# Gates taken out of the retention and made in seven products of sums of blocks, with the attention's output projection ahead of them

## The chip, the cores and the metric

The kernel runs on one core of one Trainium2 chip. The metric is the device time of one execution, in microseconds (us); a kernel's time is the median of its runs. The engines are named as in the profile: PE (TensorE matmuls) and PEld (its weight loads), DVE (VectorE), ACT (ScalarE), POOL (GpSimd) and SP (SyncE, which issues nearly all DMA transfers of this kernel, in program order).

## The reference

One layer of a hybrid model: a block of neighbourhood attention and a block of retention share one input projection, each is projected back, both are merged by gates, and a gated MLP follows. Cut to the part that the change touches (1024 tokens, width 1024, 4 retention heads with values 256 wide, 1024 columns for each gate):

```python
hx = _modulate(_rmsnorm(x, norm1_g[l]), sh1, sc1)
(xq, xk, xv, xrq, xrk, xrv, xrg, xga, xgb) = jnp.split(hx @ w_in[l], IN_OFFSETS, axis=-1)
...
o_ret_x, _, _ = _bi_retention(q_r, k_r, _heads(xrv, RET_HEADS), ret_log_decay_fwd[l], ret_log_decay_bwd[l], s_f, s_b)
o_ret = _ret_output(o_ret_x, xrg)
...
merged = jax.nn.sigmoid(gate_na) * (o_na @ w_proj_na) + jax.nn.sigmoid(gate_ret) * (o_ret @ w_proj_ret)
return merged @ w_out
```

There are thus three gates, each `hx` (1024 x 1024) times a weight of 1024 x 1024: `xrg` (weight `w_rg`), with which the retention's output is multiplied after a SiLU, and `xga`, `xgb` (weight `w_gate`, branches 0 and 1), sigmoids on the two projected branches.

## The kernel before

Every operand of a matmul is held as a sum of two, high and low (`split`, L83: ACT copies to the high part, DVE subtracts for the low one), and every product is made of three matmuls: high by high, high by low, low by high (`chain`, L103, and `mm3`, L120). A weight block of 128 x 512 comes through `wload` (L95): SP loads it into one of three `raw` buffers, and `split` writes it into one of six `wc` buffers. A DMA is issued on SP in the order in which the program is written, or later where a buffer has to come free first. The tiles are given out by pools with a fixed number of buffers, and each engine works through its instructions in order.

The parts that matter here, in the order of the program:

- **Retention.** For each of the four heads there are ten `front` slots (two blocks of context, eight of tokens) that make queries, keys and values, and four `gate` slots (L1156) that make the head's gate with `w_rg`, SiLU included, into `sg`. A `slot` (L1234) issues three pieces of its main work and between them the steps of another generator: the mixing (`Mix`: `mix_a`, `mix_b`, `mix_c`) of a head whose front is complete. So a head's mixing starts in its own gate slots (three of them carry a step) and goes on in the next head's front slots. `mix_b` normalises a block of 128 tokens (bn_stats, bn_aggr and a power on POOL), `mix_c` transposes it and multiplies it by `sg`, and stores it to `d_oret` in DRAM.
- **Tail.** The last head's mixing has three gates as filler (`tail`, `gate_fill`). They are three of the eight merge gates that were made early and spilled to `d_gate`, those of the output blocks `db` 0 to 3; the other five are made during the attention.
- **Gates and projections** (L1300 to L1377). The eight remaining merge gates (`db` 4 to 7, both branches; tiles `g`), with the loads of the spilled ones between them; beside them eight transposed blocks of the attention's output (`tpn`, L1347, loaded from `d_ona`) and the generator `down_sums`, which loads 44 blocks of `w_down`, makes 44 differences on POOL (`pj`, L1317) and stores them to `d_w`. Then the attention's output projection with `w_pna` (`pn`, L1374), multiplied by its gate, and between its blocks the retention's output comes back from `d_oret` and is split to `orr` (L1370).
- **Merge.** The retention's projection with `w_pret` (`pr`, L1393), times its gate, plus the other branch. Then `w_out` and the MLP. Its up projection already uses seven products of sums of blocks in place of eight products (a class with a method `step` of seven cases).

Products with a two by two division of both operands into blocks come, in that form, as seven products instead of eight; the sums of weight blocks are made on POOL (`s1` to `s4`), those of the moving operand once (T1 to T4), and those of the results when they leave PSUM.

## Time and profile before

| | us |
|---|---|
| median of three runs | 1797.33 (1794.11 and 1798.88 the others) |
| profiled execution, its own time | 1797.5 |
| span of the profiled execution, first to last instruction | 1795.7 |
| mean granted clock of TensorE over the span | 0.990 |

Busy time of the engines in the stretches that the change rebuilds, and the share of the DMA engines' time:

| stretch (us from the start of the span) | PE | DVE | ACT | POOL | granted clock | DMA |
|---|---|---|---|---|---|---|
| 470 to 813, retention from the second head to the end of its tail | 343.00 | 208.46 | 131.61 | 77.50 | 1.00 | 0.22 |
| 813 to 905, merge gates, transposes, `down_sums` | 90.90 | 14.77 | 28.11 | 52.33 | 1.00 | 0.91 |
| 905 to 949, projection `pn`, `orr` | 40.54 | 28.08 | 18.95 | 5.86 | 0.96 | 0.75 |
| 949 to 1036, projection `pr` and merge | 87.00 | 42.14 | 22.18 | 40.62 | 1.00 | 0.29 |

How to read the profile: an engine's busy time over a stretch, against the length of the stretch, says how far it is from being full there. "Idle before" of an instruction is the time for which its engine had nothing to do ahead of it, and the name behind the arrow is what ended that time. A line such as L84 is a line of the kernel; L84 and L85 are the two halves of `split`, wherever it is called.

### The profile page before, as it was taken

The numbers are of one execution on the slowest core, as the hardware profiler recorded it, in microseconds if no ns is written. First come the engines' busy times: TensorE is split into PE (matmuls) and PEld (weight loads), VectorE is DVE, ScalarE is ACT, GpSimd is POOL, SyncE is SP. The second block draws the span as 40 slices with busy tenths as digits, with TensorE's granted clock in tenths as the row PEclk, the third lists the DMA queues.
The fourth block names the chain that finished last, engine by engine and source line by source line (L and its number), as shares of the span: only waits on it lengthen the run. The fifth ranks groups of instructions, "written<-read, shape, count | busy, mean of one in ns | idle before, by whom it ended". The sixth has DMA issues, their size and how long they took to land.

```text
span 1795.7 us, 24565 instructions
## 1 busy us (share of the span) xinstructions
PE 1746.7 (97%) x8477; PEld 1450.1 (81%) x8477; DVE 1216.9 (68%) x2386; ACT 821.2 (46%) x1768; POOL 520.8 (29%) x445
## 2 busy tenths in 40 slices
PE   8799999999999999999999999989999999999997
PEld 4588888888888888888778878878888888788886
DVE  5978887765656666551254646869989989875755
ACT  5666666652524343432342223544444444554444
POOL 2600000001222212125422610065545555211444
PEclk9899999999999999999999999999999999999999
DMA  9134334330303030238982333642232233486753
GB/s 356 52 113 128 105 113 148 119 98 9 95 16 100 19 91 24 74 91 285 318 262 88 88 136 134 235 160 88 90 116 88 97 122 104 163 284 193 240 168 149
DMA packets 128031, 240.64 MB, mean 134 GB/s; under 512 B 14593, under 2 KB 27041, under 8 KB 127905
## 3 DMA queue, kind: packets, MB, share of 16 engines
q1 hardware_dynamic: 127904, 239.06, 41.0%
q8 instruction: 67, 1.10, 0.3%
q14 instruction: 60, 0.48, 0.1%
HBM read 179.48 MB, written 56.90 MB: 132 GB/s over the span
## 4 chain that ended last, share of the span: by engine, by line
PE 74%; DVE 6%; issue 6%; DMA 6%; POOL 4%; ACT 3%; SPq 1%; POOLq 0%; ACTq 0%; DVEq 0%
PE u L1628 18%; PE mm L110 5%; PE mm L111 5%; PE mm L112 5%; PE y L1628 4%; PE mm L121 4%; PE mm L123 4%; PE mm L122 4%; PE R L509 2%; PE ptp L491 2%; PE om L121 1%; PE om L122 1%; PE om L123 1%; DVE wc L85 1%; DMA raw<-in_w_out 1%
## 5 line engine op out<-in xcount | busy, mean ns | idle before, releaser
L1628 PE MATMUL u<-T,wc 128*128 128x512 f32 x960 | 227.0, 392 | 5.3 <-ACT pu L1605 5.0
L1628 PEld LDWEIGHTS u<-T,wc 128*128 128x128 f32 x960 | 180.5, 189 | 46.3 <-ACT pu L1605 8.8
L1628 PE MATMUL y<-wc,ahl 128*128 128x512 f32 x924 | 212.2, 392 | 3.3 <-DVE wc L85 1.8
L1628 PEld LDWEIGHTS y<-wc,ahl 128*128 128x128 f32 x924 | 174.5, 189 | 40.8 <-DVE wc L85 2.5
L111 PE MATMUL mm<-low,wc 128*128 128x512 f32 (+1 forms) x456 | 174.1, 382 | 0.0
L85 DVE TENSOR_TENSOR wc<-ur,wc 128x512 fp32r<-128x512 f32 x137 | 122.6, 896 | 66.3 <-ACT wc L84 66.3
L110 PE MATMUL mm<-hx,wc 128*128 128x512 f32 x392 | 157.8, 403 | 0.3 <-DVE vc L219 0.3
L85 DVE TENSOR_TENSOR wc<-raw,wc 128x512 fp32r<-128x512 f32 x140 | 104.8, 753 | 75.5 <-ACT wc L84 75.1
L112 PE MATMUL mm<-hx,wc 128*128 128x512 f32 x392 | 155.1, 396 | 0.0
L84 ACT CAST wc<-ur 128x512 fp32r<-128x512 f32 x137 | 85.1, 622 | 129.7 <-PE y L1628 72.1
L84 ACT CAST wc<-raw 128x512 fp32r<-128x512 f32 x140 | 86.8, 621 | 72.5 <-DMA raw<-in_w_gate 22.6
L1628 PE MATMUL u<-h2a,wc 128*128 128x512 f32 x480 | 112.3, 389 | 0.7 <-DVE pu L1613 0.7
L1628 PEld LDWEIGHTS u<-h2a,wc 128*128 128x128 f32 x480 | 90.0, 188 | 19.8 <-DVE pu L1613 1.1
L111 PEld LDWEIGHTS mm<-low,wc 128*128 128x128 f32 x456 | 86.1, 189 | 11.3
L84 ACT CAST wc<-s 128x512 fp32r<-128x512 f32 x80 | 49.6, 622 | 91.9 <-PE u L1628 87.0
L123 PE MATMUL mm<-wc,low 128*128 128x512 f32 (+1 forms) x240 | 91.2, 380 | 0.0
L85 DVE TENSOR_TENSOR wc<-s,wc 128x512 fp32r<-128x512 f32 x80 | 83.4, 1044 | 3.7 <-ACT wc L84 3.4
L112 PEld LDWEIGHTS mm<-hx,wc 128*128 128x128 f32 x392 | 73.8, 188 | 13.6
L110 PEld LDWEIGHTS mm<-hx,wc 128*128 128x128 f32 x392 | 73.9, 189 | 12.1 <-PE c L123 0.7
L1351 POOL TENSOR_TENSOR col<-col,bcol 128x32 f32<-128x32 f32 x1 | 0.3, 253 | 281.6 <-DVE aw L536 281.6
L121 PE MATMUL mm<-wc,hx 128*128 128x512 f32 x192 | 75.2, 392 | 0.7 <-ACT r L1103 0.7
L122 PE MATMUL mm<-wc,hx 128*128 128x512 f32 x192 | 75.1, 391 | 0.0
(380 smaller groups left out, 4424.6 us busy)
## 6 DMA issues: line engine op xcount, KB each, us to landing
ur<-in_w_up SPq DMA_DIRECT2D x80, 256.0 KB, 2.8
ur<-d_a SPq DMA_DIRECT2D x77, 256.0 KB, 3.2
aw<-in_w_ada SPq DMA_DIRECT2D x32, 512.0 KB, 3.3
pj<-in_w_down SPq DMA_DIRECT2D x44, 256.0 KB, 4.6
d_w<-pj SPq DMA_DIRECT2D x44, 256.0 KB, 4.3
d_a<-sa SPq DMA_DIRECT2D x44, 256.0 KB, 2.0
ur<-d_w SPq DMA_DIRECT2D x44, 256.0 KB, 3.9
d_a<-at SPq DMA_DIRECT2D x33, 256.0 KB, 2.6
```

The costliest lines, as they stand in the source:

```text
L84: act.copy(hi, src)
L85: (lo_eng or vec).tensor_tensor(lo, src, hi.bitcast(F32), ALU.subtract)
L110: pe.matmul(out, wh, xh, start=k == 0, stop=False)
L111: pe.matmul(out, wh, xl, start=False, stop=False)
L112: pe.matmul(out, wl, xh, start=False, stop=k == n - 1)
L121: pe.matmul(out, ah, bh, start=first, stop=False)
L122: pe.matmul(out, ah, bl, start=False, stop=False)
L123: pe.matmul(out, al, bh, start=False, stop=last)
L491: pe.transpose(tp[:, c], self.Pm[h][:, c * P : (c + 1) * P], ident)
L509: pe.matmul(R[:, h], self.pair.V[:, g, h].rearrange("p a b -> p (a b)"), self.PT[h][:, c].rearrange("p a b -> p (a b)"), start=c == 0, sto ...
L1351: pool.tensor_tensor(col[:, 16:48], col[:, 16:48], bcol[:, 16:48], ALU.add)
L1628: pe.matmul(out, a, b, start=first and n == 0, stop=last and n == 2, skip_group_check=True)
```

## The change

The retention no longer makes its gates: `gate` is gone, `mix_c` copies the transposed block to DRAM as it is, and the mixing of a head rides along in slots 1 to 9 of the next head's front and slot 0 of the one after. `v` gets buffers of its own for the context blocks (`c0`, `c1`). The filler of the tail comes in pieces of six matmuls instead of nine (`STEP`).

Behind the retention come, in this order: the eight transposes `tpn`; the attention's output projection `pn` for all eight `db`, stored to a new `d_pn` (times the gate for `db` 0 to 3, whose gates were spilled, without it for `db` 4 to 7), and beside it `hx_sums`, which forms the sums T1 to T4 of the blocks of `hx` on POOL and DVE and splits them; then the class `Gates`, eight units of seven products of twelve matmuls each: four retention heads (`ret`, `w_rg`) and the merge gates of `db` 4 to 7 (`merge`, `w_gate`, both branches in one unit). The steps of neighbouring units are interleaved, and `down_sums` advances at every fifth step. A unit's results go through SiLU or sigmoid, are multiplied by the retention's output from `d_oret` or the projection from `d_pn` where that applies, and are stored to `d_orr`, `d_pn` or `d_gate`. Behind the units, 16 tiles of `d_orr` are loaded and split to `orr`, and 16 tiles each of `d_pn` and `d_gate` loaded to `sg`. The projection with `w_pret` and all behind it are as before. The up projection's class becomes `Up`, with the common part in `Seven`; its instructions and their order stay.

PE has 8463 instructions before and 8367 after, ACT 1600 and 1673, DVE 2348 and 2412, POOL 450 and 498, SP 866 and 946.

PE, end of the retention, before: the last transposes of the mixing (`tpo`) stand among matmuls of a spilled gate (`mm`) and the first merge gate (`g`).

```order
L111 MATMUL mm_8855<-low_595,wc_8785 128x512
L112 MATMUL mm_8855<-hx0_91,wc_8785 128x512
L1207 MATMUL tpo_8886<-ident_74,o_8739 128x128 x2
L110 MATMUL mm_8855<-hx0_91,wc_8785 128x512
L111 MATMUL mm_8855<-low_580,wc_8785 128x512
L112 MATMUL mm_8855<-hx0_91,wc_8785 128x512
L110 MATMUL mm_8855<-hx0_91,wc_8785 128x512
L111 MATMUL mm_8855<-low_698,wc_8785 128x512
L112 MATMUL mm_8855<-hx0_91,wc_8785 128x512
L1207 MATMUL tpo_8901<-ident_74,o_8816 128x128 x2
L110 MATMUL g_8973<-hx0_91,wc_8965 128x512
```

PE at the same place after the change (line numbers of the changed kernel): the last mixing blocks (`O`, `tpo`), the transposes of the attention's output (`tpn`), and behind eight of these the projection (`pn`).

```order
L1199 MATMUL tpo_8299<-ident_76,o_8167 128x128 x2
L123 MATMUL O_8305<-v_7080,A_8276 128x256
L124 MATMUL O_8305<-v_7080,A_8276 128x256
L125 MATMUL O_8305<-v_7080,A_8276 128x256
L1199 MATMUL tpo_8317<-ident_76,o_8230 128x128 x2
L1199 MATMUL tpo_8323<-ident_76,o_8284 128x128 x2
L1317 MATMUL tpn_8357<-ident_76,raw_8355 128x128 x4
L1317 MATMUL tpn_8366<-ident_76,raw_8364 128x128 x4
L1317 MATMUL tpn_8375<-ident_76,raw_8373 128x128 x4
```

The matmuls of gates that stood between and behind the last transposes have moved to the units behind the projection.

SP at the start of the units, after the change: the last results of the projection (`pn`), the store of `d_ada`, the four weight blocks of the first unit (`wr`) and the first load of `down_sums`.

```order
L1337 DMA d_pn_62<-pn_8767 128x512
L1337 DMA d_pn_62<-pn_8800 128x512
L1337 DMA d_pn_62<-pn_8816 128x512
L1347 DMA d_ada_60<-arow_8833 32x128
L1442 DMA wr_8841<-in_w_rg 128x512
L1442 DMA wr_8843<-in_w_rg 128x512
L1442 DMA wr_8845<-in_w_rg 128x512
L1442 DMA wr_8847<-in_w_rg 128x512
L1418 DMA pj_8910<-in_w_down 128x512
```

The stores are new, and the weights of `w_rg`, which before were loaded within the retention, stand behind them.

SP ahead of the projection with `w_pret`, before: each block of `w_pna` is followed by two loads of the retention's output, and the last two by the first blocks of `w_pret`.

```order
L89 DMA raw_10031<-in_w_pna 128x512
L89 DMA raw_10036<-d_oret_58 128x512
L89 DMA raw_10040<-d_oret_58 128x512
L89 DMA raw_10072<-in_w_pna 128x512
L89 DMA raw_10077<-d_oret_58 128x512
L89 DMA raw_10081<-d_oret_58 128x512
L89 DMA raw_10120<-in_w_pret 128x512
L89 DMA raw_10125<-in_w_pret 128x512
```

SP after the change, from the store of the last unit (`c_10238`):

```order
L1472 DMA d_pn_62<-c_10238 128x512
L91 DMA raw_10309<-d_orr_63 128x512
L91 DMA raw_10313<-d_orr_63 128x512
L1504 DMA sg_10379<-d_gate_61 128x512
L91 DMA raw_10317<-d_orr_63 128x512
L1502 DMA sg_10362<-d_pn_62 128x512
L91 DMA raw_10321<-d_orr_63 128x512
L91 DMA raw_10325<-d_orr_63 128x512
```

The same pattern goes on (12 loads from `d_orr` behind that store in all, with 7 to `sg` between them); behind it stand 20 more loads to `sg`, and then:

```order
L1502 DMA sg_10425<-d_pn_62 128x512
L1504 DMA sg_10427<-d_gate_61 128x512
L1511 DMA gate1_10432<-d_ada_60 128x1024
L91 DMA raw_10434<-in_w_pret 128x512
L91 DMA raw_10439<-in_w_pret 128x512
```

All of the retention's output, the projected branch and the gates is thus loaded between the last unit and the first block of `w_pret`.

The diff, cut to its core:

```diff
+    d_pn = dram.tile([KB, 2, P, 512], F32, name="d_pn")
+    d_orr = dram.tile([RH * 2, P, T], F32, name="d_orr")
...
-            vtag = self.order[i] if i < NCB else tb
+            vtag = f"c{i}" if i < NCB else tb
...
-        def gate(self, half, b):
-            if not half and not b:
-                self.sg = rt.tile([P, 2, T], F32, tag="sg", bufs=1, name="sg")
-                self.h0 = self.back[0] // 4
-            half = half ^ self.h0
-            wg = [wload(io["w_rg"][self.h, b, i]) for i in range(2)]
-            m = mm_tile()
-            yield from chain(m, wg, hxs(0, half), hxs(1, half), 3)
-            act.activation(self.sg[:, b, half * 512 : (half + 1) * 512], m, AF.Silu)
...
-            vec.tensor_tensor(ot, tp, self.sg[:, :, tb * P : (tb + 1) * P], ALU.mult)
+            act.copy(ot, tp)
...
-            slot(head.front(i), mix if mix and not mix.done() else None, head if i else None, i - 1)
+            slot(head.front(i), mix, *last)
+            if i == 0:
+                mix = Mix(last[0]) if h else None
+            last = (head, i)
...
-        mix = Mix(head)
-        last = (head, NCB + NTB - 1)
-        for n, (half, b) in enumerate(((0, 0), (0, 1), (1, 0), (1, 1))):
-            slot(head.gate(half, b), mix if n else None, *(last if n == 0 else ()))
...
-    STEP = 3
+    STEP = 2
...
+    slot(pieces3(tl), mix, *last)
+    mix = Mix(head)
     while not mix.done():
         slot(pieces3(tl), mix)
...
-        if g in spilled:
-            for half in range(2):
-                t = sg[g][half]
-                sync.dma_start(t, d_gate[g[0] * 2 + g[1], half])
-                act.activation(t, t, AF.Sigmoid)
-        else:
-            wg = [wload(io["w_gate"][g[0], g[1], i]) for i in range(2)]
-            for half in range(2):
-                m = g_ps("g")
-                mm_a(m, wg, hxs(0, half), hxs(1, half))
-                act.activation(sg[g][half], m, AF.Sigmoid)
-            next(down_sums)
...
+    def hx_sums(k):
+        b = {}
+        for i, half in ((0, 1), (0, 0), (1, 1), (1, 0)):
+            kb, c0 = k + KH * i, half * 512
+            b[i, half] = t = onap.tile([P, 512], F32, tag="b", bufs=8, name="b")
+            pool.tensor_tensor(t, hxp(0, kb, c0, 512).bitcast(F32), hxp(1, kb, c0, 512).bitcast(F32), ALU.add)
+        b11, b12, b21, b22 = b[0, 0], b[0, 1], b[1, 0], b[1, 1]
+        for c, o, x, y in (("T1", b11, b12, b11), ("T3", b12, b22, b12), ("T2", b22, b22, b11), ("T4", b21, b21, b22)):
+            vec.tensor_tensor(o, x, y, ALU.subtract)
+        yield
+        for c, src in (("T2", b22), ("T1", b11), ("T3", b12), ("T4", b21)):
+            split(hxT[c][0][:, k], hxT[c][1][:, k], src)
...
+    for db in range(KB):
+        wp = [wload(io["w_pna"][db, 0])]
+        hs = hs if db % 2 else hx_sums(db // 2)
+        for half in range(2):
+            sl_ = slice(half * 512, half * 512 + 512)
+            m = g_ps("pn")
+            mm_a(m, wp, lambda k: ona[0][:, k, sl_], lambda k: ona[1][:, k, sl_])
+            t = onap.tile([P, 512], F32, tag="pn", bufs=3, name="pn")
+            if (db, 0) in spilled:
+                g = onap.tile([P, 512], F32, tag="sg", bufs=2, name="sgt")
+                sync.dma_start(g, d_gate[2 * db, half])
+                act.activation(g, g, AF.Sigmoid)
+                vec.tensor_tensor(t, m, g, ALU.mult)
+            else:
+                act.copy(t, m)
+            sync.dma_start(d_pn[db, half], t)
+        next(hs)
...
+    def open3(out, ah, al, bh, bl, first, last):
+        for n, (a, b) in enumerate(((ah, bh), (ah, bl), (al, bh))):
+            pe.matmul(out, a, b, start=first and n == 0, stop=last and n == 2, skip_group_check=True)
+    class Seven:
+        def load(self):
+            self.a21, self.a22, self.a11, self.a12 = [self.raw(self.src[b, i]) for b, i in ((1, 0), (1, 1), (0, 0), (0, 1))]
+            self.s1, self.s2, self.s3, self.s4 = (self.raw(None) for _ in range(4))
+            pool.tensor_tensor(self.s1, self.a21, self.a22, ALU.add)
+            pool.tensor_tensor(self.s2, self.s1, self.a11, ALU.subtract)
+            pool.tensor_tensor(self.s3, self.a11, self.a21, ALU.subtract)
+            pool.tensor_tensor(self.s4, self.a12, self.s2, ALU.subtract)
+        def prod(self, bank, a, c, first, last):
+            w = wtile()
+            split(w[:, 0], w[:, 1], a)
+            for k, (xh, xl) in enumerate(self.moving(c)):
+                open3(bank, w[:, 0, k * P : (k + 1) * P], w[:, 1, k * P : (k + 1) * P], xh, xl, first and k == 0, last and k == KH - 1)
+        def add(self, b, half, bank, x):
+            vec.tensor_tensor(self.dst(b, half), bank, x, ALU.add)
+            self.done(b, half)
+        def step(self, n):
+            if n == 0:
+                self.load()
+                self.banks()
+                self.p1, self.u2, self.u3 = (self.tmp() for _ in range(3))
+                self.prod(self.X, self.a11, "B11", True, False)
+                act.copy(self.p1, self.X)
+            elif n == 1:
+                self.prod(self.Y, self.s2, "T2", True, False)
+                vec.tensor_tensor(self.u2, self.Y, self.p1, ALU.add)
+            elif n == 2:
+                self.prod(self.Z, self.s1, "T1", True, False)
+            elif n == 3:
+                self.prod(self.Y, self.s3, "T3", False, False)
+                vec.tensor_tensor(self.u3, self.Y, self.p1, ALU.add)
+                self.add(1, 1, self.Z, self.u3)
+            elif n == 4:
+                self.prod(self.X, self.a12, "B21", False, True)
+                self.c11()
+            elif n == 5:
+                self.prod(self.Y, self.a22, "T4", False, True)
+                self.add(1, 0, self.Y, self.p1)
+            else:
+                self.prod(self.Z, self.s4, "B22", False, True)
+                self.add(0, 1, self.Z, self.u2)
...
+    def interleaved(n0, n):
+        return [(i, k) for _, i, k in sorted((7 * i + 2 * k, i, k) for i in range(n0, n) for k in range(7))]
...
+        def __init__(self, kind, n):
+            self.kind, self.n = kind, n
+            w = io["w_rg" if kind == "ret" else "w_gate"]
+            self.src = {(b, i): w[n, b, i] for b in range(2) for i in range(2)}
+            self.c = {}
+        def raw(self, src):
+            t = gr.tile([P, 512], F32, tag="r", bufs=10, name="wr")
+            if src is not None:
+                sync.dma_start(t, src)
+            return t
...
+        def banks(self):
+            self.X, self.Y, self.Z = (g_ps("u") for _ in range(3))
...
+        def done(self, b, half, t=None, src=None):
+            t = self.c[b, half]
+            src, n, cs = t if src is None else src, self.n, slice(half * 512, half * 512 + 512)
+            act.activation(t, src, AF.Silu if self.kind == "ret" else AF.Sigmoid)
+            if self.kind == "ret" or b == 0:
+                o = gr.tile([P, 512], F32, tag="o", bufs=2, name="o")
+                sync.dma_start(o, d_oret[2 * n + b, :, cs] if self.kind == "ret" else d_pn[n, half])
+                vec.tensor_tensor(t, t, o, ALU.mult)
+            sync.dma_start(d_orr[2 * n + b, :, cs] if self.kind == "ret" else d_pn[n, half] if b == 0 else d_gate[2 * n + 1, half], t)
+    nsp = len(spilled) // 2
+    gu = [Gates("ret", h) for h in range(RH)] + [Gates("merge", db) for db in range(nsp, KB)]
+    for n, (i, k) in enumerate(interleaved(0, len(gu))):
+        gu[i].step(k)
+        if n % 5 == 2:
+            next(down_sums, None)
+    for _ in down_sums:
...
     orr = {(half, k): [orp.tile([P, 512], F32R, name=f"orr{half}_{k}_{i}") for i in range(2)] for half in (1, 0) for k in range(2 * RH)}
+    for half in range(2):
+        for db in range(KB):
+            split(*orr[half, db], rawload(d_orr[db, :, half * 512 : half * 512 + 512]))
+    sg = {}
     for db in range(KB):
-        wp = [wload(io["w_pna"][db, 0])]
         for half in range(2):
-            split(*orr[half, db], rawload(d_oret[db, :, half * 512 : half * 512 + 512]))
-        for half in range(2):
-            sl_ = slice(half * 512, half * 512 + 512)
-            m = g_ps("pn")
-            mm_a(m, wp, lambda k: ona[0][:, k, sl_], lambda k: ona[1][:, k, sl_])
-            g = sg[db, 0][half]
-            vec.tensor_tensor(g, m, g, ALU.mult)
-        next(down_sums, None)
-    wsp.release()
-    onap.release()
+            sg[db, 0, half] = gtile(half, F32, "sg")
+            sync.dma_start(sg[db, 0, half], d_pn[db, half])
+            sg[db, 1, half] = t = gtile(half, F32, "sg")
+            sync.dma_start(t, d_gate[2 * db + 1, half])
+            if (db, 1) in spilled:
+                act.activation(t, t, AF.Sigmoid)
```

171 lines of the change are left out of this document (80 added, 91 removed).

## The prediction

> **What bounds the kernel now.** I read the page first, then the order of PE's work around the rebuilt stage, then its waits and its busy time by stretch.
>
> ```profile
> PE 1746.7 (97%) x8477; PEld 1450.1 (81%) x8477; DVE 1216.9 (68%) x2386; ACT 821.2 (46%) x1768; POOL 520.8 (29%) x445
> PE 74%; DVE 6%; issue 6%; DMA 6%; POOL 4%; ACT 3%; SPq 1%; POOLq 0%; ACTq 0%; DVEq 0%
> ```
>
> TensorE (PE) is busy 97% of the span and holds most of the chain that ended last. So a matmul that goes is worth one step of PE, and each microsecond in which PE has no work costs one. The next rows give the step, and what a pause does to it (columns: start, duration, engine and line; in brackets the idle time before).
>
> ```profile
> 915.73 0.39 PE L111 MATMUL pn<-ona,wc 128*128 128x512 f32 x1
> ...
> 916.64 0.39 PE L112 MATMUL pn<-ona,wc 128*128 128x512 f32 x1
> 919.89 0.64 PE L110 MATMUL pn<-ona,wc 128*128 128x512 f32 x1 [2.87 <-ACT wc L84]
> 920.34 0.63 PE L111 MATMUL pn<-ona,wc 128*128 128x512 f32 x1
> PE pn L110 <- ACT wc L84: 3.5, 2, 2.9
> PE g L110 <- ACT wc L84: 1.1, 1, 1.1
> 920.00:940.00 20.00, 20.00 (x81) 16.18 (x82) 12.83 (x20) 7.85 (x13) 0.00 (x0) 0.91 0.66 204
> ```
>
> From 915.73 to 916.64 lie four steps: 0.2275 us for 512 columns. Behind a pause of 2.87 us the step is 0.45, and the granted clock of those 20 us is 0.91: 9% of 20 = 1.8 us more for a pause of that length. I charge 1.8 for a longer one too; only this pause is shown. Between 800 and 950 us PE waited 3.5 + 1.1 us, for weights.
>
> The sum is made against the profiled execution, 1797.5 us (span 1795.7 and 1.8 around it); the median of the three runs, 1797.33, is the same within 0.01%.
>
> **What goes.** Four gate slots of 24 matmuls per head, and four pairs of merge gates of 96, are 8 x 96 = 768 matmuls. Seven products of 12 for each of the eight units are 672. The 96 between them, at 0.2275, are 21.8 us, all of it where PE is the bound. The waits of 4.6 us and their 1.8 of slow clock belong to code that is rewritten. Together **28.2 us**, if nothing is late next.
>
> **What comes,** in the order of the program; each step is a time in which PE has nothing to do.
>
> (a) Retention. The gate slots gave a head's last mixing steps cover, and the next head's weights time to come. Now every front slot carries a mixing step.
>
> ```profile
> 680.00:700.00 20.00, 20.00 (x109) 17.20 (x108) 14.52 (x54) 7.11 (x22) 7.34 (x11) 1.00 0.07 21
> ```
>
> This stretch is front and mixing together (columns: PE, weight loads, DVE, ACT, POOL, clock, DMA): PE full, VectorE (DVE) at 73%, and one of DVE's products per step now goes to ScalarE (ACT), at 36%. PE stays the bound there. At three head boundaries some of the next head's eight weight blocks wait for buffers of the last head. From 0, if the slack holds, to 5, a wait like the 1.1 to 2.9 above at each boundary; I take 1.5, nearer to the row that shows slack.
>
> (b) End of retention. In before, matmuls of a spilled gate and of the first stage gate stand around the last transposes of the mixing (first fence on the order); now there is nothing but mixing, eight transposes of the attention output and the first projection.
>
> ```profile
> 802.83 0.28 PE L123 MATMUL O<-v,A 128*128 128x256 f32 x1
> 803.15 0.42 DVE L1194 TENSOR_TENSOR o<-O,o 128x256 f32<-128x256 f32 x1 [3.04 <-PE O L123]
> 805.63 0.41 DVE L1201 TENSOR_SCALAR o<-o,mvr 128x256 f32<-128x256 f32 x1 [0.44 <-POOL mvr L1200]
> raw<-in_w_rg SPq DMA_DIRECT2D x32, 256.0 KB, 2.7
> L84 ACT CAST orr<-raw x16: 614/620/627, 905.6 to 940.1; 128x512 fp32r<-128x512 f32 x16
> L85 DVE TENSOR_TENSOR orr<-raw,orr x16: 684/692/1790, 906.2 to 940.8; 128x512 fp32r<-128x512 f32 x16
> ```
>
> From a block's last matmul to its normalised rows are 3.2 us (802.83 to 806.04). The last two blocks do this one behind the other without filler, about 6.3 from the last filler matmul to the last transposes. Their stores stand on SyncE (SP), in front of the fourth load of d_ona: loads four to six go out at 7.4 to 8.2 and land 2.7 later. The three raw buffers then come free one by one for loads seven and eight and for the first projection's weights; these land near 13.5, 14.2 and 14.9, those of the second block near 16.7. With a cast of 0.62, PE runs densely from 17.5. Its own work until then is 7.7. Wait 10, slow clock 1.8: **11.8**. Ends: 8, if the two chains do not disturb each other, and 17, if the new POOL sums hold DVE up.
>
> (c) Start of the products. On SP the first weights of the products stand behind the store of the last projection and of d_ada (second fence), so they are asked for only when the projections have ended.
>
> ```profile
> L1358 ACT COPY arow<-tpa x1: 236/236/236, 905.4 to 905.4; 32x128 f32<-32x128 f32 x1
> ```
>
> The last projection's copy (0.6 as the cast above), the copy of arow (0.24), and four issues of some 0.35 put the third load, a11, which the first product needs, at 2.3; 2.7 to land and 0.65 of queue behind its fellows, the cast 0.62: 6.1, and 1.8 of slow clock: **7.9**. Ends: 5 without queue and slow clock, 11 if stores that are still under way add three transfers.
>
> (d) Inside the products. 672 x 0.2275 = 152.9 us of PE. DVE has 40 results from PSUM at 0.69 (28 us) and 80 operations with two SBUF inputs at 0.69 (55); POOL 32 sums for weights and 44 differences at 1.32 (100). The nearest row is a stretch of the up projection, which has this form already:
>
> ```profile
> L1317 POOL TENSOR_TENSOR pj<-pj 128x512 f32<-128x512 f32 x44 | 58.2, 1324 | 54.8 <-DMA pj<-in_w_down 48.9 <-POOL pj L1317 2.0 <-DMA d_w<-pj 1.9
> L85 DVE TENSOR_TENSOR wc<-s,wc 128x512 fp32r<-128x512 f32 x80 | 83.4, 1044 | 3.7 <-ACT wc L84 3.4
> 1200.00:1500.00 300.00, 299.66 (x1316) 246.09 (x1315) 264.62 (x264) 134.84 (x187) 162.47 (x94) 1.00 0.32 103
> ```
>
> There PE is full, with DVE at 88% and POOL at 54%; here DVE has 54% and POOL 65%. I take 3, from 0 (that row) to 12 (four waits like 2.87: one pair of bursts of the weight sums, which now share POOL with the differences, held up twice).
>
> The Trainium skill ("SBUF — State Buffer", section "SBUF: two separate sides") says that a DVE operation with two SBUF inputs and a GpSimd operation that reads SBUF hold a shared port pair one at a time, the other fully blocked. It speaks against placing the differences beside the products: by it the stage would take 183 us (second rival), by the row 156. The trace agrees with it in part: the splits beside POOL take 1044 ns, those of orr 692.
>
> (e) The refill before w_pret. In before the orr loads stand between projections, and the weights of w_pret right behind the last of them (third fence). Now the gated products go to d_orr, d_pn and d_gate, and come back through SP after the last unit's store; that store needs the last product, a DVE addition 0.69, an activation 0.59 and a product 0.69, with splits between: 2.9 after the last matmul. Behind it on SP stand 12 of the 16 d_orr loads (3 buffers), 27 loads into sg, gate1, and then the first weights.
>
> ```profile
> L1341 ACT ACTIVATE sg<-g x16: 577/586/598, 813.9 to 904.9; 128x512 f32<-128x512 f32 x16
> L1395 DVE TENSOR_TENSOR sg<-pr,sg x16: 675/688/692, 954.5 to 1045.6; 128x512 f32<-128x512 f32 x16
> 938.71 10.28 SPq L89 DMA_DIRECT2D raw<-in_w_pret  x8
> 887.09 0.33 SPq L1334 DMA_DIRECT2D sg<-d_gate  x1
> 887.73 1.67 SPq L1315 DMA_DIRECT2D d_w<-pj  x3
> 889.80 0.33 SPq L89 DMA_DIRECT2D raw<-in_w_pna  x1
> 880.00:900.00 20.00, 20.00 (x90) 16.51 (x89) 1.62 (x3) 5.72 (x11) 11.72 (x9) 1.00 0.99 351
> ```
>
> Eight loads on three buffers take 10.28, 7 steps in 9.95: 1.42 each. So the 12th is issued at 2.9 + 11 x 1.42 = 18.5 and lands near 21.5; the 7 sg loads between them fit in the gaps. Then 20 sg loads, gate1 (512 KB, as two) and the first w_pret stand in the queue. From 887.09 to 889.80 four transfers of 256 KB go out in 2.71, 0.68 each, in a stretch in which DMA is busy 99% at 351 GB/s. 23 x 0.68 = 15.6: landing at 37.2, cast 0.62: PE idles 38, with slow clock **39.8**. Ends: 34 (all 42 transfers at 0.68 from 2.9 on, latency and cast behind), and 46 (the sg loads between the 12 do not fit in the gaps, 7 x 0.68 = 5, and a queue in front).
>
> The sum: 1.5 + 11.8 + 7.9 + 3 + 39.8 = 64.0, less 28.2: **+35.8**, 1797.5 + 36 = **1834** (rounded). All low ends: 47 - 28.2 = +18.8, 1816. All high ends: 91 - 28.2 = +62.8, 1860.
>
> **Rivals.**
>
> 1. The other side: the refill hides under the last products, faster than before. Stores and loads of units one to seven could run ahead, and only the last tile would be late; then (e) is nearly 0 and, with the other terms at their low ends (0 + 8 + 5 + 0), 1797.5 - 28.2 + 13 = **1782**. It decides as soon as (e) is under 28.2 - 24.2 = 4 us (24.2: the other terms as I take them). For it: DMA is busy 32% in the up stretch. Against it: SP issues in program order, 40 loads stand behind a store that needs the last product. Chance 0.05.
>
> 2. DVE and POOL exclude each other in the products. If none of the 55 us with two SBUF inputs lies beside POOL's 100, the stage needs 55 + 28 + 100 = 183 against 152.9: 30 more in place of the 3 of (d), so 1834 + 27 = **1861**. For it: 1044 against 692. Against: PE at 299.66 of 300 in the up stretch, with 264.62 + 162.47 = 427 us on the two engines, so they do run side by side much of the time. Chance 0.10.
>
> 3. Retention loses its cover: some 30 slots that now carry both works each wait 0.7 (a DVE operation of a mixing step that comes late), 21 us: **1855**. For: DVE at 73% in bursts. Against: PE full there. Chance 0.07.
>
> That the change does not do what it says is out: the order has 96 matmuls of 512 columns fewer.
>
> **How the numbers follow.** Forecast, 1834 from its own ends 1816 to 1860: 0.76. Rivals 0.05, 0.10, 0.07; 0.02 for the rest. The range goes from just below the low ends, **1814**, just beyond the second rival, **1862**; what it leaves out is the first rival and a combination of two late cases. A measurement of this kernel can tell about 0.3% (5.4 us) from no change. Faster: the first rival without its part near no change, **0.03**. Same: **0.03** (that part, and a refill at half its price with all other low ends). Slower: **0.94**.
>
> **What would show it.** In the profile of the changed kernel: 96 PE matmuls fewer; before the first product of w_pret one pause of some 38 us, ended by a cast of weights that a DMA released; some 10 us of PE's idle time at the first projections, 6 before the first product; granted clock below 1 right behind each; PE full in between, with the stage of products near 156 us. Wrong would be: a short pause before w_pret (the loads ran ahead: rival 1); PE with many small idle times among the products that DVE or POOL ended (rival 2); the same in the heads (rival 3).

## The result, and the profile after

| | us |
|---|---|
| changed kernel, median of four runs | 1845.34 (1843.57 to 1849.32) |
| kernel before, median of four runs beside it | 1797.74 (1794.11 to 1798.88) |
| ratio | 1.0271, 95% interval 1.0249 to 1.0294 |
| profiled executions, after and before | 1843.57 and 1797.5 |

The change makes the kernel 2.7% slower. From the page of the changed kernel, its busy times:

```profile
PE 1736.1 (94%) x8381; PEld 1436.4 (78%) x8381; DVE 1314.1 (71%) x2450; ACT 852.6 (46%) x1841; POOL 604.0 (33%) x493
```

PE is 10.6 us less busy and the span 45.7 us longer: PE stands more. The waits of PE in the changed kernel, first at the end of the retention (720 to 742 us), then in the rebuilt stage (786 to 1000 us); columns: who waited for whom, total us, times, longest:

```profile
PE tpn L1317 <- DMA raw<-d_ona: 3.3, 4, 1.2
PE tpo L1199 <- DVE mvr L1191: 2.6, 1, 2.6
PE tpo L1199 <- DVE o L1193: 1.8, 1, 1.8
PE pn L112 <- ACT wc L86: 1.7, 1, 1.7
PE pr L112 <- ACT wc L86: 42.6, 1, 42.6
PE u L1356 <- ACT wc L86: 7.0, 1, 7.0
PE u L1356 <- DVE pu L1391: 2.4, 1, 2.4
```

Nearly all of it lies at the three boundaries between stages: 9.4 us at the end of the retention (the last transposes of the mixing, those of the attention's output, and the first projection), 7.0 before the first product, 42.6 before w_pret. Among the products themselves PE waits 2.4. SP's row in the longest pause, after the last matmul of the products, which starts at 952.85 (the issue of each transfer; a row with x2 or x3 is so many in a line):

```profile
955.79 0.32 SPq L1472 DMA_DIRECT2D d_pn<-c  x1
956.20 0.91 SPq L91 DMA_DIRECT2D raw<-d_orr  x2
...
974.98 0.32 SPq L91 DMA_DIRECT2D raw<-d_orr  x1
975.35 0.42 SPq L1502 DMA_DIRECT2D sg<-d_pn  x1
...
987.81 0.32 SPq L1504 DMA_DIRECT2D sg<-d_gate  x1
...
989.20 1.68 SPq L91 DMA_DIRECT2D raw<-in_w_pret  x3
```

The last unit's store goes out 2.9 us after the last product, the last of twelve loads of the retention's output at 974.98, the twentieth load to sg at 987.81, and only then the weights for which PE waits. This is the row that the fences on the order promised. The clock behind the pauses, in the windows that follow the first projections, the first product and the first matmul of w_pret (columns as in the prediction, the clock third from the end):

```profile
740.00:760.00 20.00, 19.41 (x72) 15.33 (x73) 17.06 (x24) 10.43 (x20) 9.68 (x7) 0.83 0.59 172
794.00:804.00 10.00, 9.27 (x26) 6.92 (x27) 7.35 (x6) 3.95 (x7) 9.69 (x7) 0.63 0.98 346
996.00:1006.00 10.00, 10.00 (x38) 8.09 (x39) 4.37 (x7) 3.39 (x6) 1.29 (x1) 0.84 0.51 157
```

The slow clock cost 17% of 20, 37% of 9.3 and 16% of 10: 3.4, 3.4 and 1.6 us.

### The profile page after: what moved, and what is told of

Same layout as the page of the kernel before. It is cut to its first block, busy times and chain, and to the rows that moved or that the text cites. A ratio compares the mean times of both kernels' runs of the same rounds, so it can differ in the third digit from the quotient of the medians.

```text
span 1841.4 us, 24786 instructions
## 1 busy us (share of the span) xinstructions
PE 1736.1 (94%) x8381; PEld 1436.4 (78%) x8381; DVE 1314.1 (71%) x2450; ACT 852.6 (46%) x1841; POOL 604.0 (33%) x493
## 4 chain that ended last, share of the span: by engine, by line
PE 71%; DVE 9%; issue 7%; DMA 6%; POOL 4%; ACT 3%; SPq 1%; POOLq 0%; ACTq 0%; DVEq 0%
PE u L1356 24%; PE y L1356 4%; PE mm L112 3%; PE mm L113 3%; PE mm L114 3%; PE mm L124 3%; PE mm L125 3%; PE mm L123 3%; PE R L511 2%; DVE wc L87 2%; PE ptp L493 2%; PE pr L112 1%; PE pr L113 1%; PE pr L114 1%; PE om L123 1%
## 5 line engine op out<-in xcount | busy, mean ns | idle before, releaser
L113 PE MATMUL mm<-low,wc 128*128 128x512 f32 (+1 forms) x328 | 124.0, 378 | 0.0
L112 PE MATMUL mm<-hx,wc 128*128 128x512 f32 x264 | 107.2, 406 | 0.3 <-DVE vc L221 0.3
L114 PE MATMUL mm<-hx,wc 128*128 128x512 f32 x264 | 105.1, 398 | 0.0
L87 DVE TENSOR_TENSOR wc<-wr,wc 128x512 fp32r<-128x512 f32 x56 | 69.9, 1255 | 36.0 <-ACT wc L86 35.6
L1356 PE MATMUL u<-hxT,wc 128*128 128x512 f32 x384 | 90.4, 391 | 2.4 <-DVE pu L1391 2.4
L112 PE MATMUL pr<-orr,wc 128*128 128x512 f32 x128 | 50.7, 396 | 42.6 <-ACT wc L86 42.6
L87 DVE TENSOR_TENSOR wc<-raw,wc 128x512 fp32r<-128x512 f32 x92 | 70.5, 775 | 24.1 <-ACT wc L86 23.8
L1356 PEld LDWEIGHTS u<-hxT,wc 128*128 128x128 f32 x384 | 72.5, 189 | 17.9 <-issue 2.8
L86 ACT CAST wc<-raw 128x512 fp32r<-128x512 f32 x92 | 57.1, 622 | 43.6 <-DMA raw<-in_w_pret 16.1
L1362 POOL TENSOR_TENSOR s<-ur 128x512 f32<-128x512 f32 x20 | 36.9, 1844 | 121.0 <-DVE wc L87 70.5
```

The costliest lines, as they stand in the source:

```text
L86: act.copy(hi, src)
L87: (lo_eng or vec).tensor_tensor(lo, src, hi.bitcast(F32), ALU.subtract)
L112: pe.matmul(out, wh, xh, start=k == 0, stop=False)
L113: pe.matmul(out, wh, xl, start=False, stop=False)
L114: pe.matmul(out, wl, xh, start=False, stop=k == n - 1)
L1356: pe.matmul(out, a, b, start=first and n == 0, stop=last and n == 2, skip_group_check=True)
```

## The experiments

My theory: PE loses at three boundaries, each by a queue or a chain of transfers that no matmul covers, and loads put in another place bring it back. The rivals: the products are bound by DVE and POOL, or by something else that moves with them. The order on each engine is settled when the program is built; the builder also moves a load ahead of or behind its place in the text, and an edit among the products can change the order on other engines too, from there to the end of the stage (that of run 7 does on ScalarE and SP; that of run 6 takes POOL's differences out and leaves the other engines' order as it was). So a run can differ from its neighbour by more than its edit, and waits of a few us among the products may come of that alone; no run tests this. Times below are medians, ratios are against the kernel before on the same chip (1800.4 to 1801.4 us there).

**1. Gate loads behind the weights of w_pret.**

```diff
         wp = [wload(io["w_pret"][db, i]) for i in range(2)]
+        sg_load(db)
+        if db == 1:
+            brow(0, gate1)
```

> The loads of the gates and projections for the merge are moved behind the weights of w_pret in the program, so that only the 12 loads of the retention's output stand between the last unit's store and those weights. If the pause of 42.6 us before w_pret is the length of the load queue: 20 loads at 0.68 us less, so a pause near 25 us, time near 1827 us. Rival, the pause is the freeing and splitting of the retention tiles, with the queue beside it: pause and time as in the changed kernel, 1845 us.

Measured: 1828.79 us, ratio 1.0142 (1.0111 to 1.0174). The longest of PE's waits in this run:

```profile
PE pr L112 <- ACT wc L86: 26.6, 1, 26.6
```

The pause falls from 42.6 to 26.6, and the time with it (by 16.6 us between the medians; by the ratios, 1.0271 and 1.0142, by some 23). Of the 27 loads to sg behind the last unit's store two still go out ahead of w_pret, and the load of gate1; the 25 others were 16 us of the pause: the queue is shown.

**2. hx free early, retention's output through the buffers of the differences.** The last ten steps become:

```diff
+    seq7 = interleaved(0, len(gu))[:-10] + [(L, 0), (L - 1, 4), (L, 4), (L - 1, 5), (L - 1, 6), (L, 6), (L, 1), (L, 2), (L, 3), (L, 5)]
...
+        if n % 4 == 2:
+            next(down_sums, None)
...
+            t = gr.tile([P, 512], F32, tag="pj", bufs=8, name="po")
+            sync.dma_start(t, d_orr[db, :, half * 512 : half * 512 + 512])
+            split(*orr[half, db], t)
+        if half == 0:
+            wp0 = [wload(io["w_pret"][0, i]) for i in range(2)]
```

> As the run with late gate loads, and besides the last two units take their products with blocks of hx first, so that hx is free four products (10.9 us) before the end, and the retention's output is loaded through the eight free buffers of the weight differences (these advance at every fourth step instead of fifth). If the pause is the wait for hx's space and then for a queue on three buffers: a pause of 2 to 5 us, time near 1806 us. Rival, the reordered last products wait for their weight sums on POOL: the pause goes but new waits of 10 us and more stand among the last products, time near 1818 us.

Measured: 1831.65 us, ratio 1.0160 (1.0136 to 1.0185).

```profile
PE u L1356 <- ACT wc L86: 22.5, 6, 6.7
PE u L1356 <- DVE pu L1391: 4.0, 2, 2.9
PE u L1356 <- ACT pu L1383: 2.3, 1, 2.3
```

No wait for w_pret is left. The rest of that pause was the space of hx, the three buffers, and the place of the first block of w_pret, whose weights now stand behind the first eight of the 16 loads; the run does not separate these. But 28.8 us stand before and among the products (22.5, 4.0 and 2.3), 6.5 of them before the first. Most of the others lie between 831 and 936 us, ahead of the reordered steps, so not where the rival put them; only the 2.3 stand among those, at 963 us.

**3. The same with differences at every fifth step** (and the loads through the buffers of the unit weights, tag "r").

```diff
-        if n % 4 == 2:
+        if n % 5 == 2:
```

> As the run with hx freed early, but the weight differences advance at every fifth step again, and the retention's output comes through the ten buffers of the unit weights. If the waits of 22 us among the products of that run came of the denser differences (POOL and its loads and stores in SP's row): waits of 2 to 6 us among the products as in the changed kernel, pause before w_pret under 6 us, time near 1810 us. Rival, they came of where the unit's stores stand in SP's row ahead of the next weights, which any new order upsets: waits of 12 us and more, time 1820 to 1832 us.

Measured: 1803.88 us, ratio 1.0018 (0.9999 to 1.0037).

```profile
PE u L1356 <- ACT wc L86: 7.5, 1, 7.5
PE u L1356 <- DVE pu L1391: 3.4, 2, 2.1
PE u L1356 <- ACT orr L86: 1.5, 1, 1.5
```

Among the products 4.9 us remain and the pause before w_pret is gone: of the 2.7% lost, 2.5 are won back. The buffers changed too, so the density of the differences is the likely cause of most of the 22 us among the products in run 2, not a shown one.

**4. First unit's weights ahead.**

```diff
+        if db == KB - 1:
+            pre = [rawload(io["w_rg"][0, b, i]) for b, i in ((0, 0), (1, 0), (1, 1))]
...
+    gu[0].a11, gu[0].a21, gu[0].a22 = pre
+    gu[0].a12 = gu[0].raw(gu[0].src[0, 1])
```

> Three of the first unit's four weight blocks are loaded through the free raw buffers during the last projection. If the 7.0 us before the first product are the request behind the last stores: the first product follows at once, the second waits 1 to 2 us for its sum on POOL, some 3 us of slow clock go too, time near 1837 us. Rival, the sums on POOL set the start: the wait only moves to the second product, 5 us or more, time above 1842 us.

Measured: 1856.41 us, ratio 1.0303 (1.0280 to 1.0325), not faster than the changed kernel (the intervals overlap). The pause before the first product is gone, but among the products PE now waits (787 to 960 us):

```profile
PE u L1358 <- ACT wc L86: 10.6, 3, 7.3
PE u L1358 <- DVE pu L1394: 5.7, 4, 2.8
```

The longest, 7.3 us, is for a weight that SP asked for late. SP's row there:

```profile
821.52 1.58 SPq L1423 DMA_DIRECT2D d_w<-pj  x3
831.41 0.32 SPq L1475 DMA_DIRECT2D d_orr<-c  x1
...
841.47 1.00 SPq L1445 DMA_DIRECT2D wr<-in_w_rg  x2
```

SP stood 8.3 us at a unit's store, whose product on DVE was late, and the next unit's weights stand behind that store. From 786 to 960 us SP waited 51.6 us at the units' stores for products on DVE, against 25.5 in the changed kernel.

**5. The start ahead, without the differences** (the blocks of w_down go to DRAM as they are).

```diff
-                pool.tensor_tensor(ts[o], ts[x], ts[y], ALU.subtract)
```

> The run with the first unit's weights ahead, without the 44 differences on POOL (the blocks of w_down go to DRAM as they are; all loads and stores stay). If the 16.7 us of waits among the products of that run came of POOL and DVE holding each other up: they fall under 4 us, and the time is 1831 to 1838 us, as the start's saving is now kept. Rival, SP standing at a store with the next weights behind it: waits of 10 us and more stay, time 1845 us or more.

Measured: 1845.62 us, ratio 1.0247 (1.0225 to 1.0269). PE's waits over the same stretch (all but 0.6 us):

```profile
PE u L1358 <- ACT wc L86: 4.7, 3, 2.5
```

16.3 us (10.6 and 5.7) became 4.7: the differences on POOL made most of the waits of run 4. They can do so by slowing DVE (run 6) or by holding SP's row, in which their loads and stores stand; the run does not separate the two. The time is 10.8 us under run 4, about what these waits would give, yet 8 to 15 above what was expected of it. The reason shows beside run 6, the same without the weights ahead: there PE waits 6.5 us before the first product and 0.6 behind it, so most of that pause is not saved here either but comes back as waits for weights. What is saved, some 2 us, two executions of each (1843.94 and 1847.30 here) can't tell from none.

**6. The changed kernel without the differences** (the edit of run 5 alone).

> The changed kernel without the 44 differences on POOL among the products (the blocks of w_down go to DRAM as they are, so what the down projection reads are other numbers); all loads and stores stay. If POOL and DVE block each other there: the splits of unit weights fall from a mean of 1255 ns to 700 to 950 ns, and the wait of 2.4 us among the products goes; as PE hides the rest, the time falls by 0 to 4 us only, to 1841 to 1845 us. Rival, the slow splits are not POOL's doing: their mean stays above 1150 ns.

Measured: 1844.97 us, ratio 1.0255 (1.0211 to 1.0299). PE's waits before and among the products (780 to 970 us):

```profile
PE u L1356 <- ACT wc L86: 6.5, 1, 6.5
PE u L1356 <- DVE wc L87: 0.6, 1, 0.6
```

The wait of 2.4 us among the products of the changed kernel is gone. Its splits of unit weights have a median of 693 ns against 1181, and its DVE is busy 23 us less over the same stretch. First the changed kernel (790 to 965 us, groups on DVE by shape: busy, mean ns; then 794 to 953 us: PE, weight loads, DVE, ACT, POOL), then this run:

```profile
L87 DVE TENSOR_TENSOR wc<-wr,wc 128x512 fp32r<-128x512 f32 x56 | 69.9, 1255 | 36.0 <-ACT wc L86 35.6
L1471 DVE TENSOR_TENSOR c<-c,o 128x512 f32<-128x512 f32 x24 | 30.4, 1267 | 9.6 <-ACT c L1467 5.5 <-DMA o<-d_oret 4.0
L1374 DVE TENSOR_TENSOR c<-u,pu 128x512 f32<-128x512 f32 x24 | 16.3, 680 | 8.8 <-PE u L1356 8.7
...
794.00:953.00 159.00, 155.90 (x672) 127.90 (x672) 119.87 (x118) 56.86 (x99) 118.16 (x75) 0.98 0.83 289
```

```profile
L87 DVE TENSOR_TENSOR wc<-wr,wc 128x512 fp32r<-128x512 f32 x56 | 51.6, 929 | 37.0 <-ACT wc L86 36.5
L1470 DVE TENSOR_TENSOR c<-c,o 128x512 f32<-128x512 f32 x24 | 20.2, 842 | 15.7 <-ACT c L1466 9.0 <-DMA o<-d_oret 4.1 <-DMA d_w<-pj 1.5
L1374 DVE TENSOR_TENSOR c<-u,pu 128x512 f32<-128x512 f32 x24 | 16.5, 687 | 18.2 <-PE u L1356 18.1
...
794.00:953.00 159.00, 155.80 (x672) 127.94 (x672) 96.59 (x121) 61.24 (x101) 46.91 (x32) 0.97 0.85 294
```

The operations with two inputs in SBUF are slowed by POOL (1255 to 929, 1267 to 842, with 32 sums on POOL still there), those with one input in PSUM (u) are not: 680 and 687. The time stays, since PE hid nearly all of it. The Trainium skill ("SBUF — State Buffer", section "SBUF: two separate sides") says that a DVE operation with two SBUF inputs and a GpSimd operation that reads SBUF take a shared pair of ports in turn, and that the later one is fully blocked. The trace agrees on which operations are slowed, 1255 against 929 ns with two inputs in SBUF and 680 against 687 with one in PSUM; that one of the two is fully blocked no run here shows.

**7. Fewer matmuls** (one product of each unit keeps 1 of its 12).

```diff
+            if c == "T1" and isinstance(self, Gates):
+                xh, xl = self.moving(c)[0]
+                pe.matmul(bank, w[:, 0, 0:P], xh, start=first, stop=last, skip_group_check=True)
+                return
```

> The changed kernel with one of the seven products of each unit cut to 1 of its 12 matmuls (it leaves out 88 matmuls of the product of S1 and T1; the gates then hold other numbers); sums, splits, loads and stores stay. If PE sets the pace among the products: 88 x 0.2275 = 20.0 us less, time near 1825 us. Rival, DVE, POOL or the loads set it: the time stays within 5 us of 1845 us and PE waits that much more.

Measured: 1862.40 us, ratio 1.0352 (1.0308 to 1.0396): neither. With 20 us of PE's work gone the kernel is some 15 us slower than the changed one (0.0081 in the ratio).

```profile
PE pr L112 <- ACT wc L86: 49.0, 1, 49.0
PE u L1356 <- ACT wc L86: 22.7, 5, 7.1
```

The units' weights come late five times (22.7 us; the 7.1 before the first product are one of them, 7.0 in the changed kernel and there the only one), and the pause before w_pret is 6 us longer. The built order differs from the changed kernel's through the whole stage; whether this order or the shorter time between the steps makes the waits stays open. So these 88 matmuls less, in the order that was built with them, bought no time; more the run does not show.

**8. Filler behind the mixing** (`STEP = 1` in the tail).

> The filler of the retention's tail comes in pieces of three matmuls instead of six, so 48 of its matmuls (10.9 us) stand behind the last transposes of the mixing. If the six pauses there (9.3 us) are missing work for PE: they fall to 1 to 3 us, the slow clock behind them goes too, time near 1835 us. Rival, the mixing's own chain sets the end and now has less cover in each slot: the pauses turn up between the mixing steps instead, time 1843 us or more.

Measured: 1846.80 us, ratio 1.0248 (1.0221 to 1.0274): no gain that can be told. First PE's waits, then SP's, from 714 to 745 us:

```profile
PE tpn L1317 <- DMA raw<-d_ona: 3.3, 2, 2.2
PE tpn L1317 <- DVE ona L1320: 2.9, 2, 1.5
PE pn L112 <- ACT wc L86: 1.2, 1, 1.2
PE tpo L1199 <- DVE o L1193: 0.9, 1, 0.9
```

```profile
SPq L91 <- PE tpn L1317: 8.4, 6, 4.8
```

The waits between the mixing's transposes (2.6 and 1.8) fall to 0.9, but the waits for the blocks of d_ona stay (3.3) and 2.9 us for their splits are new. The fourth load waits for the first transpose to free one of the three raw buffers, and that transpose now stands behind the filler. Neither theory had that. The buffers alone are not the limit either: run 9 below gives five of the eight blocks space of their own, with the filler as in the changed kernel, and PE still waits 9.1 us at this boundary (2.7, 1.5 and 4.9), since the loads then stand behind the mixing's stores in SP's row. Both together were not run.

**9. All of it, with the units' stores on ScalarE's queue** (runs 3 and 4, five blocks of d_ona loaded into the space of T2, `act.dma_start` for the stores).

> Late gate loads, hx freed early with differences at every fifth step, first unit weights ahead, five of the eight d_ona blocks loaded into the space of T2, and the units' results stored through ScalarE's queue instead of SP's. If the waits among the products are SP standing at a store with the next weights behind it: waits under 6 us there, pause before w_pret under 6 us, 2 us before the products, 8 us at the end of the retention, time 1796 to 1803 us, about that of before. Rival, the loads themselves or the engines set them: 12 us and more among the products, time 1812 us or more.

Measured: 1807.79 us, ratio 1.0036 (1.0018 to 1.0054).

```profile
PE u L1362 <- DVE pu L1398: 5.7, 2, 2.9
PE u L1362 <- ACT pu L1390: 4.7, 1, 4.7
PE u L1362 <- DVE pu L1393: 4.0, 3, 3.0
PE u L1362 <- ACT wc L86: 2.9, 3, 1.3
```

17.3 us among the products (5.7, 4.7, 4.0 and 2.9), the rival's sign, at a time between the two forecasts. PE now waits mostly for results on DVE and ACT, not for weights. The stores did not stop holding up an engine: ScalarE's casts of unit weights wait 29.2 us (13 times, never in the changed kernel) for the products on DVE whose stores ScalarE now issues ahead of them, and SP waits 31.8 us for the same products at the loads of `o`, whose two buffers they free. DVE's products are late; the edit moved the standing from one engine to another.

**10 to 12. Some of the differences moved beside w_pret.** Five of eleven groups there (run 10), the same with the first weights ahead (run 11), two groups with the weights ahead (run 12, whose edit is shown).

```diff
-        if n % 5 == 2:
-            next(down_sums, None)
+        if n % 6 == 2 and n < 54:
+            next(down_sums)
...
+        if db in (2, 4):
+            next(down_sums, None)
```

> The run with hx freed early and differences at every fifth step, with six of the eleven groups of differences left among the products (at every ninth step) and five moved beside the projection with w_pret, where POOL has room (39 of 88 us; 20 more at 1.32 are 26). If POOL and DVE among the products cost what is left of waits there: waits among the products from 5 us to 2 or less, nothing lost beside w_pret, time 1797 to 1801 us against 1804 of that run. Rival, the differences delay the merge's own sums on POOL or the weights in SP's row: new waits beside w_pret, time 1805 us or more.

> As the run with half the differences, and the first unit's weights ahead. If the start's pause moved into the products only because POOL, DVE and the loads had no slack there, it is saved now: 7 us and some 3 us of slow clock less, time 1788 to 1794 us, 0.4 to 0.7% under the kernel before. Rival, the products take the same time from their first request for weights whatever else is moved: the waits turn up among the products, time 1800 us or more.

> As the run with half the differences and the first weights ahead, with nine of the eleven groups of differences among the products (every sixth step) and two beside the projection with w_pret (before its third and fifth block). That run lost 12 us at w_pret (99.0 against 87.0 in the kernel before) and 8 in the output projection, where its five groups delay weights in SP's row and sums on POOL. If that loss goes with the number of groups: 3 to 6 us of it stay, the products wait 2 to 4 us, time 1793 to 1800 us, at or under the kernel before. Rival, three groups more among the products bring their waits back (16.7 us in the run with all of them and the weights ahead): time 1805 us or more.

Measured: 1817.04 us, ratio 1.0087 (1.0073 to 1.0101); 1810.21, 1.0046 (1.0032 to 1.0061); 1800.95, 1.0003 (0.9990 to 1.0016). In run 11 PE waits 1.5 us among the products, and the weights ahead are worth 7 us against run 10; but beside w_pret and in the output projection (935 to 1070 us) it waits 12.2 us, as run 10 did (10.9), where the kernel before waits 3.6. The three longest:

```profile
PE pr L112 <- ACT wc L86: 3.8, 1, 3.8
PE om L123 <- ACT wx L86: 2.2, 1, 2.2
PE om L125 <- DVE ml L87: 1.9, 1, 1.9
```

Run 12, with nine groups among the products (780 to 1070 us):

```profile
PE om L123 <- ACT mh L86: 5.7, 1, 5.7
PE u L1358 <- DVE pu L1394: 4.1, 2, 2.9
PE u L1358 <- ACT wc L86: 2.9, 2, 1.7
```

All three missed what was expected of them: run 10 came out as its rival said, run 11 at its rival's time but with the waits elsewhere, run 12 between the two. Run 12 takes what the kernel before takes, no less: the loss is won back, and of the 28.2 us that the change could bring nothing is left over. Where the 21.8 us of the matmuls went can be estimated: from 700 to 1100 us PE waits 21.7 us in run 12 and 8.2 in the kernel before, 13.5 more; the retention costs 3.4 (term (a) below); and the clock is 0.57 over 730 to 750 us, 43% of the 13.8 that PE works there, 6.0. These are 22.9, less the 1.8 of slow clock that the kernel before has. No version of these beats the kernel before.

## Why the prediction came out as it did

Direction and range were right (1845 in 1814 to 1862), the size was short: +46.1 us between the profiled executions, +35.8 forecast. By its own terms:

| term | forecast | measured |
|---|---|---|
| matmuls and waits that go | -28.2 | -28.2 (96 matmuls by count, the waits gone; not measured by itself) |
| (a) retention | 1.5 | 3.4 |
| (b) end of the retention, idle | 10 | 9.4 |
| (c) start of the products, idle | 6.1 | 7.0 |
| (d) inside the products | 3 | 2.4 |
| (e) refill, idle | 38 | 42.6 |
| slow clock behind (b), (c), (e) | 5.4 | 8.4 |
| sum | 35.8 | 45.0 |

1.1 of the 46.1 us is left over. Term (a) comes from the first and last slot of the retention, in the kernel before and in the changed one:

```profile
L1099 DVE TENSOR_TENSOR v<-mm,v x40: 411/423/425, 396.4 to 738.3; 128x256 fp32r<-128x256 f32 x40
```

```profile
L1101 DVE TENSOR_TENSOR v<-mm,v x40: 411/423/425, 397.8 to 677.6; 128x256 fp32r<-128x256 f32 x40
```

From 341.9 us to 279.8 are 62.1 less, where twelve gate slots of 24 matmuls are 65.5. So (a) landed inside its ends of 0 and 5, but by luck: it was to be waits at the head boundaries, and over these stretches PE is without work for 1.0 us before (busy 340.87 of 341.90) and 1.3 after (278.46 of 279.80). The other 3 us are lost while PE is busy; why stays open.

- **(e)** held in mechanism and place; run 1 shows the loads to sg, and in runs 2 and 3 the rest goes too. It was undersized mostly because the twelve loads did not go out every 1.42 us: from 956.20 to 974.98 are 11 steps of 1.71, so the last goes out 22.1 us after the last product and not 18.5. The loads to sg between them were counted as fitting into gaps; they share the queue, the retention's loads land after a median of 4.1 us (2.8 for the w_pret loads behind the 1.42), and the three buffers come back later for it. Run 1 bears this out: its last six loads of the retention's output, with no other load between them, go out every 1.42 us (972.82 to 979.90). The rest is the first block of w_pret, which at the end of the full queue took 6.0 us to land. This is the case that the upper end of 46 was for.
- **The slow clock** was one price for every pause, from one pause of 2.87 us. It was 3.4, 3.4 and 1.6, 8.4 in place of 5.4; the longest pause has the smallest.
- **(b)** was right in size. Its explanation (work missing) was part of it at most: run 8 moves the work there and gains nothing that can be told, since the loads of d_ona on three buffers come late as well, which the working had; and with buffers but no filler the wait stays too (run 9).
- **(c) and (d)** were right as numbers and wrong as a picture. I treated the start and the products as two costs. Run 4 removes the first and gets it back, and more, as the second. Without the differences it comes back too, 5.3 us of waits in run 5 against 7.1 in run 6. So most of the 7 us at the start was probably slack in which the weights of later units came in time, and the differences make the return larger. (d) also took DVE at 54% of the stage; it was 75% (119.87 of 159), as its operations on two SBUF inputs took 1.26 us and not 0.69.
- **Rival 2** (DVE and POOL exclude each other): that they slow each other is a fact here by run 6; full exclusion isn't shown. It cost the changed kernel the wait of 2.4 us at most, not 30. With all differences among the products, weights ahead cost time (run 4); with five of eleven groups moved out they paid 7 us (run 11); with none at all they paid nothing that can be told (run 5). Why run 11 and run 5 differ stays open.
- **Rival 1** (the refill hides) needed SP to load ahead, and hx's space stood against it besides. Here it took other last steps, other buffers and another order of loads together (run 3), and then the kernel is about as fast as before, not 1782: the other terms stay.
- **Rival 3** is out: 3.4 us against 21.
- The term -28.2 rests on a matmul being worth its step. That was read off the kernel before, where PE is busy 90.90 of 92 us in its stage of gates; for the products run 7 did not bear it out, in an order of its own.

## What to carry to other kernels

Count what a saving of matmuls makes the other engines and the queue do in the same stretch: here 21.8 us of PE were bought with 64 more DVE operations, 32 sums on POOL that share a stretch with 44 others, and some 80 more transfers. Where results leave through DRAM and come back, ask what stands in the issuing engine's row between the last store and the first weight behind it; move what is needed last behind what is needed first (run 1, an order of loads, took 16 us off the pause). And when a pause is removed and the time does not fall, look for it further on: it may have been slack in which later loads came in time.

## What the runs showed of the hardware

- What a pause costs in slow clock does not go by its length here. After 42.64 us without work the first steps were slow and cost 1.6 us (window 996 to 1006, clock 0.84); after 7.04 us the cost was 3.4 (window 794 to 804, clock 0.63); after the 2.37 us at 855 it was nothing that the windows show, and after the 2.87 us in the kernel before 1.8. It is no fixed price either: behind nearly the same pauses at the end of the retention (9.4, 9.0 and 9.0 us in all) the clock over 720 to 760 us was 0.87, 0.79 and 0.70 in the changed kernel, run 6 and run 5.
- A DVE operation on two tiles in SBUF took 1.7 times as long with POOL busy 118 of 159 us as with 47 (medians 1181 and 693 ns); one with an input in PSUM took the same (680 and 687 on average).
- With the queue full a transfer of 256 KB went out every 0.68 us (981.04 to 987.81 are ten steps) and landed 5.4 us later (columns: KB each, median us to landing), twice the 2.7 of the loads of w_rg in the kernel before:

```profile
sg<-d_pn SPq DMA_DIRECT2D x16, 256.0 KB, 5.4
```
